# Decoder block on one core: the DMAs of the delta heads' inversion move to GpSimd's queue

## Chip, core and metric

The kernel runs on one core of a Trainium2 chip. The metric is the device time of one execution in microseconds (us), lower is better; a run's number here is a median over runs. TensorE (PE) multiplies, VectorE (DVE), ScalarE (ACT) and GpSimd (POOL) work elementwise, and SyncE (SP) only issues DMAs. Each engine, and each engine's DMA queue, takes its instructions in order.

## What is computed

A decoder block on x of 1024 tokens and 1024 channels in float32: a half step of a gated feed-forward network, a mixer, a second such half step, a final norm. The mixer adds two kinds of attention. The change touches one, the gated delta rule with 8 heads of 128 channels:

```
G = jnp.cumsum(scalar_chunks(g.astype(f32)), axis=-1)
decay = jnp.exp(jnp.where(causal, G[..., :, None] - G[..., None, :], -jnp.inf))
kk = jnp.einsum("bhnid,bhnjd->bhnij", k_beta, k) * decay
M = jnp.eye(CHUNK, dtype=f32) + jnp.where(strict, kk, 0.0)
sol = lax.linalg.triangular_solve(M, rhs, left_side=True, lower=True, unit_diagonal=True)
qk = jnp.einsum("bhnid,bhnjd->bhnij", q, k) * decay
def step(S, xs):
    qdc, qkc, uc, wc, kc, gc = xs
    v_new = uc - jnp.einsum("bhcd,bhdv->bhcv", wc, S)
    o = jnp.einsum("bhcd,bhdv->bhcv", qdc, S) + jnp.einsum("bhij,bhjv->bhiv", qkc, v_new)
    S = S * gc[..., None, None] + jnp.einsum("bhcd,bhcv->bhdv", kc, v_new)
    return S, o
```

The triangular solve is done by inverting M.

## The kernel before

Feed-forward products and projections are three matmuls each of float32 split in a high and a low part (L138, L367). After the first feed-forward step comes the mixer, with the eight delta heads in a loop over i (ORDER gives the head), then the other attention, whose gates also use the delta heads' results (y_d), then the second feed-forward step.

A delta head treats its 1024 tokens as 8 blocks of 128 on the partitions. Its steps, by the names in the code:

- `delta_kq`, `delta_v`: projections of k, q and v with a short convolution. Their matmuls (L138) are the bulk of TensorE's work in a head, and other steps are woven between them.
- `delta_decay`: loads the head's row of cumulated decay from g_d to all partitions (gb, 512 KB, two buffers, by SyncE) and makes from it em, the decay matrix (one buffer). L845 is VectorE's first step that reads gb.
- `delta_prep`: products of k with k and q (L902). VectorE multiplies them with em (L904 gives qk, L908 the triangle, written over em). SyncE stores the 32 x 32 diagonal blocks in l_d (4 DMAs, L914), loads them with one block row per partition as lt (4 DMAs, L917) and loads the identity xp (L919). GpSimd inverts all 32 blocks in 31 steps of two operations (L924, L927), copies the result transposed (xt, L929), and stores xp and xt in x_d (4 DMAs each, L932 and L933).
- `delta_blocks`: SyncE loads the inverses back in place as xb and yb (8 DMAs, L944 and L945).
- `delta_levels`: TensorE joins the 32 x 32 inverses to those of the whole block (L981, L994); it needs xb and yb.
- `delta_rec`: the recurrence over the 8 blocks, with the output norm (`out_rms`, L800 to L806) and the output oT (L1040). L1040 reads a PSUM bank that a later product needs. qsq of L967 belongs to this norm.

The loop works ahead: in turn i it makes em and starts the inversion of head i + 1, and projects k and q of head i + 2. Each engine's order is settled when the program is built, by a scheduler with priorities (the tile framework); around the steps named it follows the order of the code. SyncE's queue holds the loads of projection weights (raw, two buffers, L112), the inversion's loads and stores, gb and the stores of finished heads (y_d) in one line.

Of the kernel before, what the change touches and what calls it, by code (L numbers as in the profile page):

```python
# [15 lines left out]
P = 128  # L16
T = 1024
# [719 lines left out]
def mixer(st, sto, tc, pool, start, xs, load_unit, dense, ptile, bank, rsqrt_newton, split, new_x, accumulate,  # L737
          ounits, dram, pr, ident, ones, cst, eye, wlr, win, wout, y_d, h_d, sqrt_table, strassen_products, wp, psum, divide, recent, pinned, run):
    nc = tc.nc
# [9 lines left out]
    def big(tag, bufs=None, shape=None):  # L749
        p = cur[0] if cur else me if tag in early else mb  # L750
        return p.tile(shape or [P, T], F32, name=tag, tag=tag, bufs=bufs)
# [69 lines left out]
    def delta_kq(i, a, kq=None, steps=None):  # L821
# [12 lines left out]
            conv_silu(U_DK + h, (8 + h) * 4, put(0), (6,), steps)  # L834
        return kq

    def delta_decay(i):
        h = ORDER[i]
        gb = big("gb", 2)
        nc.sync.dma_start(out=gb, in_=g_d[h:h + 1, :].broadcast_to([P, T]))  # L840
        gb4 = gb.rearrange("p (n a i) -> p n a i", n=NCH, a=2)
        gla, glb = gb4[:, :, 0, 63], gb4[:, :, 1, 63]
        db = sp.tile([P, NCH, 2], F32, name="db", tag="db", bufs=2)
        nc.vector.tensor_copy(out=db, in_=ngt[:, h, :].unsqueeze(2).broadcast_to([P, NCH, 2]))
        nc.vector.tensor_add(out=db[0:64, :, 1], in0=db[0:64, :, 1], in1=gla[0:64])  # L845
        kdec = sp.tile([P, NCH], F32, name="kdec", tag="kdec", bufs=2)
        nc.vector.tensor_add(out=kdec, in0=db[:, :, 1], in1=glb)
        nc.scalar.activation(out=kdec, in_=kdec, func=AF.Exp)
        gl = sp.tile([P, NCH], F32, name="glast", tag="glast", bufs=2)
        nc.vector.tensor_add(out=gl, in0=gla, in1=glb)  # L850
        nc.scalar.activation(out=gl, in_=gl, func=AF.Exp)
        em = big("em", 1)
        nc.vector.tensor_tensor(out=em.rearrange("p (m i) -> p m i", i=64),
                                in0=gb.rearrange("p (m i) -> p m i", i=64),
                                in1=db.rearrange("p n a -> p (n a)").unsqueeze(2).broadcast_to([P, 16, 64]),
                                op=ALU.add)
        nc.vector.tensor_tensor(out=v3(em), in0=v3(em), in1=minmask.unsqueeze(1).broadcast_to([P, NCH, P]),
                                op=ALU.min)
        nc.scalar.activation(out=em, in_=em, func=AF.Exp)
        gla_c = sp.tile([P, NCH], F32, name="glac", tag="glac", bufs=2)  # L860
        nc.vector.tensor_copy(out=gla_c, in_=gla)
        nc.vector.tensor_tensor(out=gb4[:, :, 1, :], in0=gb4[:, :, 1, :],
                                in1=gla_c.unsqueeze(2).broadcast_to([P, NCH, 64]), op=ALU.add)
        nc.scalar.activation(out=gb, in_=gb, func=AF.Exp)

        return gb, gl, kdec, em

    def delta_prep(i, kq, kdec, em, res):
        h = ORDER[i]
        kT = kq[:, :, 0, :]  # L870
        kst = big(f"kst{i % 2}", 1)
        ssk = sp.tile([P, NCH], F32, name="ssk", tag="ssk", bufs=2)
        for b in range(2):
            q = bank()
            for n in range(4):
                nc.tensor.transpose(out=q[:, n * P:(n + 1) * P], in_=kT[:, b * 4 + n, :], identity=ident)
            for n in range(4):
                c = b * 4 + n
                jk = sp.tile([P, P], F32, name="jk", tag="jk", bufs=1)
                nc.scalar.activation(out=jk, in_=q[:, n * P:(n + 1) * P], func=AF.Square,  # L880
                                     accum_out=ssk[:, c:c + 1])
            nc.vector.tensor_tensor(out=v3(kst)[:, b * 4:b * 4 + 4, :], in0=q4(q),
                                    in1=kdec[:, b * 4:b * 4 + 4].unsqueeze(2).broadcast_to([P, 4, P]), op=ALU.mult)
        nc.vector.tensor_scalar(out=ssk, in0=ssk, scalar1=EPS, scalar2=None, op0=ALU.add)
        rs = rsqrt_newton(sp, ssk, NCH, "rs", 2)
        cj = sp.tile([P, NCH], F32, name="cj", tag="cj", bufs=2)
        nc.vector.tensor_mul(out=cj, in0=rs, in1=rs)
        nc.vector.tensor_mul(out=cj, in0=cj, in1=beta[:, h, :])
        nc.vector.tensor_mul(out=rs, in0=rs, in1=ssk)

        lt3 = v3(em)
        qk = big(f"qk{i % 2}", 1)
        em3 = v3(em)
        for b in range(4):
            if b % 2 == 0:
                pin = yield
            q = bank()
            q3 = q.rearrange("p (n a i) -> p n a i", n=2, a=2)
            with pinned(pin):
                for n in range(2):  # L900
                    c = b * 2 + n
                    nc.tensor.matmul(out=q[:, n * 256:n * 256 + 256], lhsT=kT[:, c, :],  # L902
                                     rhs=kq[:, c, :, :], start=True, stop=True)
            nc.vector.tensor_tensor(out=v3(qk)[:, b * 2:b * 2 + 2, :], in0=q3[:, :, 1, :],  # L904
                                    in1=em3[:, b * 2:b * 2 + 2, :], op=ALU.mult)
            for n in range(2):
                c = b * 2 + n
                nc.vector.scalar_tensor_tensor(out=lt3[:, c, :], in0=q3[:, n, 0, :], scalar=cj[:, c:c + 1],  # L908
                                               in1=em3[:, c, :], op0=ALU.mult, op1=ALU.mult)
        l_d = dram.tile([32, 32, 32], F32, name=f"l_d{h}")  # L910
        x_d = dram.tile([2, 32, 32, 32], F32, name=f"x_d{h}")
        for b in range(4):
            r = slice(32 * b, 32 * b + 32)
            nc.sync.dma_start(out=l_d[8 * b:8 * b + 8].rearrange("n j i -> j n i"), in_=lt3[r, :, r])  # L914
        lp = big("lt", 1, [P, 32, 32])
        for a in range(4):
            nc.sync.dma_start(out=lp[32 * a:32 * a + 32], in_=l_d)  # L917
        xp = big("xp", 1, [P, 32, 8])
        nc.sync.dma_start(out=xp, in_=eye)  # L919
        for j in range(31):  # L920
            r, m = 31 - j, min(j + 1, 8)
            tmp = mp.tile([P, 256], F32, name="itmp", tag="itmp", bufs=1)
            tv = tmp[:, :r * m].rearrange("p (r c) -> p r c", r=r)
            inv_eng.tensor_tensor(out=tv, in0=lp[:, j, j + 1:].unsqueeze(2).broadcast_to([P, r, m]),  # L924
                                  in1=xp[:, j, :m].unsqueeze(1).broadcast_to([P, r, m]), op=ALU.mult)
            xv = xp[:, j + 1:, :m]
            inv_eng.tensor_tensor(out=xv, in0=xv, in1=tv, op=ALU.subtract)  # L927
        xt = big("xt", 1, [P, 256]).rearrange("p (c i) -> p c i", c=8)
        inv_eng.tensor_copy(out=xt.rearrange("p c i -> p i c"), in_=xp)  # L929
        for a in range(4):  # L930
            r, c = slice(32 * a, 32 * a + 32), slice(8 * a, 8 * a + 8)
            nc.gpsimd.dma_start(out=x_d[0, :, :, c], in_=xp[r])  # L932
            nc.gpsimd.dma_start(out=x_d[1, :, c, :], in_=xt[r])  # L933
        res[i] = (x_d, kst, qk, cj, rs)

    def delta_blocks(em, x_d):
        lt3, n13 = v3(em), v3(n1)
        nc.vector.tensor_copy(out=n13[0:32, :, 32:64], in_=lt3[0:32, :, 32:64])
        nc.vector.tensor_copy(out=n13[64:96, :, 96:128], in_=lt3[64:96, :, 96:128])
        nc.vector.tensor_copy(out=n2, in_=lt3[0:64, :, 64:128])  # L940
        xb3, yb3 = v3(xb), v3(yb)
        for b in range(4):
            r = slice(32 * b, 32 * b + 32)
            nc.sync.dma_start(out=xb3[r, :, r], in_=x_d[0, 8 * b:8 * b + 8].rearrange("n i c -> i n c"))  # L944
            nc.sync.dma_start(out=yb3[r, :, r], in_=x_d[1, 8 * b:8 * b + 8].rearrange("n i c -> i n c"))  # L945

    def delta_v(i, kq, gb, rs, res, steps):
        h = ORDER[i]
# [276 lines left out]
    for b in range(2):  # L1225
        q = bank()
        for n in range(4):
# [5 lines left out]
        nc.vector.tensor_scalar(out=ngt[:, :, b * 4:b * 4 + 4], in0=qv[:, 64:72, :], scalar1=-1.0,  # L1233
                                scalar2=None, op0=ALU.mult)

    gb, gl, kdec, em = delta_decay(0)
    kqs = [kq0]
    preps, vs = {}, {}
# [5 lines left out]
    outs = []  # L1244
    for i in range(8):
        kq, (x_d, kst, qk, cj, rs), gl0 = kqs[i], preps[i], gl
        gb0 = gb
        prep = None
        if i < 7:
            gb, gl, kdec, em = nd  # L1250
            prep = delta_prep(i + 1, kqs[i + 1], kdec, em, preps)
            next(prep)
# [5 lines left out]
            run(v)  # L1258
        qsq, vt3 = vs[i]
        yi = delta_levels()  # L1260
        if i < 7:
            delta_blocks(em, preps[i + 1][0])
        else:
            stl.close()
            stl = ExitStack()
            mx = pool(stl, "mx")
# [4 lines left out]
        for j in GATES[i]:  # L1271
            gate(U_DG + ORDER[j], U_MB + ORDER[j], outs[j])
            nc.sync.dma_start(out=y_d[ORDER[j]], in_=outs[j])
        if i < 4:
            nc.sync.dma_start(out=y_d[ORDER[i]], in_=outs[i])
    sums_own, sums_inplace, strassen = strassen_products(
        mx, xs, lambda: wp.tile([P, 512], F32, name="raw", tag="raw", bufs=2),
        lambda: wp.tile([P, 512], F32, name="raw", tag="raw", bufs=2),
# [167 lines left out]
```

## Time and profile before

| | |
|---|---|
| median of 3 runs | 2672.56 us (2671.76 to 2674.8) |
| the profiled execution | 2674.82 us, of which span 2672.4 |
| TensorE busy | 2503.4 us, 94% |
| VectorE busy | 1869.0 us, 70% |
| GpSimd busy | 1113.9 us, 42% |
| ScalarE busy | 1066.5 us, 40% |
| mean granted clock of TensorE | 0.983 |
| delta heads | from about 750 to 1340 us |

Starts and idle times below are in microseconds from the span's start. "Idle before" names what ended the wait of that engine; a chain of waits is followed back from its end. A DMA's row is its issue, and its landing comes later.

### The profile page before, as it was taken

The numbers are of one execution on the slowest core, as the hardware profiler recorded it, in microseconds if no ns is written. First come the engines' busy times: TensorE is split into PE (matmuls) and PEld (weight loads), VectorE is DVE, ScalarE is ACT, GpSimd is POOL, SyncE is SP. The second block draws the span as 40 slices with busy tenths as digits, with TensorE's granted clock in tenths as the row PEclk, the third lists the DMA queues.
The fourth block names the chain that finished last, engine by engine and source line by source line (L and its number), as shares of the span: only waits on it lengthen the run. The fifth ranks groups of instructions, "written<-read, shape, count | busy, mean of one in ns | idle before, by whom it ended". The sixth has DMA issues, their size and how long they took to land.

```text
span 2672.4 us, 32776 instructions
## 1 busy us (share of the span) xinstructions
PE 2503.4 (94%) x11656; PEld 2019.5 (76%) x11656; DVE 1869.0 (70%) x2907; ACT 1066.5 (40%) x1845; POOL 1113.9 (42%) x1200
## 2 busy tenths in 40 slices
PE   7899999899997988889989999999989999998998
PEld 6788888667776767667767787877768888886677
DVE  8755556999686767667586757766586555558996
ACT  5333334333352434344345544545233333343331
POOL 4544444653327444445452212221154444446541
PEclk9999999999998999999999999999999999999999
DMA  3222221322222222212211212122312222213222
GB/s 114 79 73 82 83 91 60 112 79 91 98 81 52 60 56 59 60 48 56 63 50 37 80 43 84 40 84 87 122 32 76 68 87 87 87 60 115 79 87 80
DMA packets 118051, 199.04 MB, mean 74 GB/s; under 512 B 37208, under 2 KB 43096, under 8 KB 117888
## 3 DMA queue, kind: packets, MB, share of 16 engines
q1 hardware_dynamic: 111376, 184.04, 21.5%
q0 software_dynamic: 4352, 10.49, 1.5%
q10 hardware_dynamic: 2160, 2.43, 0.3%
q8 instruction: 91, 1.49, 0.2%
q14 instruction: 72, 0.59, 0.1%
HBM read 158.73 MB, written 38.17 MB: 74 GB/s over the span
## 4 chain that ended last, share of the span: by engine, by line
PE 60%; DVE 16%; POOL 9%; issue 5%; DMA 4%; ACT 4%; SPq 2%; POOLq 0%; DVEq 0%; ACTq 0%
PE q L367 28%; PE m L367 10%; PE ps L138 10%; PE q L573 6%; POOL xp L927 4%; POOL itmp L924 3%; DVE wl L126 3%; DVE xl L126 1%; DVE ha L578 1%; DVE h L578 1%; PE q L902 1%; PE q L981 1%; DMA s<-a_d 1%; DVE xl L238 1%; DMA gb<-g_d 1%
## 5 line engine op out<-in xcount | busy, mean ns | idle before, releaser
L126 DVE TENSOR_TENSOR wl<-raw,wh 128x512 fp32r<-128x512 f32 x244 | 200.2, 821 | 172.0 <-ACT wh L125 170.5
L138 PE MATMUL ps<-xl,wh 128*128 128x512 f32 (+2 forms) x736 | 254.8, 405 | 20.2 <-ACT wh L119 8.3
L126 DVE TENSOR_TENSOR wl<-sr,wh 128x512 fp32r<-128x512 f32 x232 | 204.7, 882 | 76.2 <-ACT wh L125 75.9
L138 PE MATMUL ps<-xh,wh 128*128 128x512 f32 (+2 forms) x736 | 254.4, 405 | 0.0
L138 PE MATMUL ps<-xh,wl 128*128 128x512 f32 (+2 forms) x736 | 254.2, 403 | 0.1
L367 PE MATMUL q<-xh,wl 128*128 128x512 f32 x640 | 249.4, 390 | 0.0
L367 PE MATMUL q<-xh,wh 128*128 128x512 f32 x640 | 249.3, 390 | 0.0
L367 PE MATMUL q<-xl,wh 128*128 128x512 f32 x640 | 249.2, 389 | 0.0
L125 ACT CAST wh<-sr 128x512 fp32r<-128x512 f32 x232 | 143.7, 619 | 244.7 <-PE q L573 61.9
L924 POOL TENSOR_TENSOR itmp<-lt,xp 128x112 f32<-128x112 f32 (+29 forms) x248 | 114.9, 463 | 255.1 <-DMA lt<-l_d 226.1
L472 POOL TENSOR_TENSOR s<-s,ysc 128x512 f32<-128x512 f32 x80 | 112.6, 1418 | 247.8 <-ACT s L471 247.8
L125 ACT CAST wh<-raw 128x512 fp32r<-128x512 f32 x244 | 144.9, 594 | 176.2 <-PE q L367 100.5
L138 PEld LDWEIGHTS ps<-xl,wh 128*128 128x128 f32 (+1 forms) x736 | 137.8, 191 | 51.7 <-DVE xl L238 9.1
L355 POOL TENSOR_TENSOR raw<-sr 128x512 f32<-128x512 f32 x20 | 27.5, 1375 | 328.6 <-DMA sr<-in_win 235.8
L138 PEld LDWEIGHTS ps<-xh,wh 128*128 128x128 f32 (+1 forms) x736 | 138.8, 192 | 24.6 <-issue 0.8
L138 PEld LDWEIGHTS ps<-xh,wl 128*128 128x128 f32 (+1 forms) x736 | 137.4, 191 | 23.7 <-issue 1.0
L378 DVE TENSOR_TENSOR c<-c,q 128x512 f32<-128x512 f32 x120 | 82.4, 686 | 84.8 <-PE q L367 84.6
L367 PEld LDWEIGHTS q<-xl,wh 128*128 128x128 f32 x640 | 120.2, 188 | 26.2
L367 PEld LDWEIGHTS q<-xh,wl 128*128 128x128 f32 x640 | 120.1, 188 | 25.5
L367 PEld LDWEIGHTS q<-xh,wh 128*128 128x128 f32 x640 | 120.1, 188 | 25.3
L373 ACT COPY c<-q 128x512 f32<-128x512 f32 x120 | 70.5, 588 | 162.2 <-PE q L367 161.7
L927 POOL TENSOR_TENSOR xp<-xp,itmp 128x112 f32<-128x112 f32 (+29 forms) x248 | 120.9, 488 | 19.4
(483 smaller groups left out, 6780.8 us busy)
## 6 DMA issues: line engine op xcount, KB each, us to landing
sr<-in_win SPq DMA_DIRECT2D x80, 256.0 KB, 2.6
a_d<-s SPq DMA_DIRECT2D x36, 512.0 KB, 3.7
raw<-in_win SPq DMA_DIRECT2D x66, 256.0 KB, 2.6
raw<-in_d SPq DMA_DIRECT2D x56, 256.0 KB, 2.6
raw<-in_g SPq DMA_DIRECT2D x48, 256.0 KB, 2.6
s<-a_d SPq DMA_DIRECT2D x24, 512.0 KB, 4.2
sr<-in_u SPq DMA_DIRECT2D x44, 256.0 KB, 2.7
raw<-in_u SPq DMA_DIRECT2D x44, 256.0 KB, 2.6
```

The lines of the kernel that those rows point to most:

```text
L125: a = nc.scalar.copy(out=hi, in_=src)
L126: b = (eng or nc.vector).tensor_sub(out=lo, in0=src, in1=hi.bitcast(F32))
L138: mm = nc.tensor.matmul(out=ps[:m, sl], lhsT=w[:, :m], rhs=x[:, sl], start=(i == 0 and a == 0), stop=(i == n - 1 and a == 2))
L355: nc.gpsimd.tensor_tensor(out=o, in0=a, in1=b, op=op)
L367: nc.tensor.matmul(out=ps, lhsT=p[:, c], rhs=q, start=(first and k == 0 and a == 0), stop=(k == 3 and a == 2), skip_group_check=not first)
L373: marks[0] = nc.scalar.copy(out=t, in_=ps).ins
L378: marks[1] = nc.vector.tensor_add(out=t, in0=t, in1=ps).ins
L472: nc.gpsimd.tensor_mul(out=s, in0=s, in1=y)
L573: nc.tensor.matmul(out=ps, lhsT=p[:, c], rhs=q, start=(first and k == 0 and a == 0), stop=(k == 1 and a == 2), skip_group_check=not first)
L578: nc.vector.scalar_tensor_tensor(out=hd[:, sl], in0=ps, scalar=0.5, in1=hd[:, sl], op0=ALU.mult, op1=ALU.add)
L924: inv_eng.tensor_tensor(out=tv, in0=lp[:, j, j + 1:].unsqueeze(2).broadcast_to([P, r, m]), in1=xp[:, j, :m].unsqueeze(1).broadcast_to([P, ...
L927: inv_eng.tensor_tensor(out=xv, in0=xv, in1=tv, op=ALU.subtract)
```

## The change

- All DMAs around the inversion (l_d, lt, xp, xb and yb) are issued by GpSimd instead of SyncE.
- The partitions of lt, xp and xt are numbered block by block (n, a) instead of part by part (a, n), so the transposed result xt is stored by one DMA of 128 x 1 KB instead of four; xp still takes four. The input eye is laid out to match.
- gb has three buffers. Its load is a function of its own, `load_decay`, called for heads 0 and 1 ahead of the loop and for head i + 2 at the start of turn i.
- The stores of heads 0 to 3 to y_d move from the end of a turn to the next turn, behind `delta_levels`.
- The scratch that the program sets aside for GpSimd's DMAs is set to 2048 bytes.

```
+    def load_decay(i):
+        h = ORDER[i]
+        gbs[i] = big("gb", 3)
+        nc.sync.dma_start(out=gbs[i], in_=g_d[h:h + 1, :].broadcast_to([P, T]))
     def delta_decay(i):
-        gb = big("gb", 2)
-        nc.sync.dma_start(out=gb, in_=g_d[h:h + 1, :].broadcast_to([P, T]))
+        gb = gbs.pop(i)
...
-            nc.sync.dma_start(out=l_d[8 * b:8 * b + 8].rearrange("n j i -> j n i"), in_=lt3[r, :, r])
+            nc.gpsimd.dma_start(out=l_d[8 * b:8 * b + 8].rearrange("n j i -> j n i"), in_=lt3[r, :, r])
...
-            nc.sync.dma_start(out=lp[32 * a:32 * a + 32], in_=l_d)
+            nc.gpsimd.dma_start(out=lp[a::4], in_=l_d)
...
-        nc.sync.dma_start(out=xp, in_=eye)
+        nc.gpsimd.dma_start(out=xp, in_=eye)
...
         for a in range(4):
-            r, c = slice(32 * a, 32 * a + 32), slice(8 * a, 8 * a + 8)
-            nc.gpsimd.dma_start(out=x_d[0, :, :, c], in_=xp[r])
-            nc.gpsimd.dma_start(out=x_d[1, :, c, :], in_=xt[r])
+            nc.gpsimd.dma_start(out=x_d[0, :, :, 8 * a:8 * a + 8], in_=xp[a::4])
+        nc.gpsimd.dma_start(out=x_d[1].rearrange("n (a c) i -> (n a) (c i)", a=4), in_=xt.rearrange("p c i -> p (c i)"))
...
-            nc.sync.dma_start(out=xb3[r, :, r], in_=x_d[0, 8 * b:8 * b + 8].rearrange("n i c -> i n c"))
-            nc.sync.dma_start(out=yb3[r, :, r], in_=x_d[1, 8 * b:8 * b + 8].rearrange("n i c -> i n c"))
+            nc.gpsimd.dma_start(out=xb3[r, :, r], in_=x_d[0, 8 * b:8 * b + 8].rearrange("n i c -> i n c"))
+            nc.gpsimd.dma_start(out=yb3[r, :, r], in_=x_d[1, 8 * b:8 * b + 8].rearrange("n c i -> c n i"))
...
+    load_decay(0)
+    load_decay(1)
...
+        if i < 6:
+            load_decay(i + 2)
...
         yi = delta_levels()
+        if 0 < i < 5:
+            nc.sync.dma_start(out=y_d[ORDER[i - 1]], in_=outs[i - 1])
...
-        if i < 4:
-            nc.sync.dma_start(out=y_d[ORDER[i]], in_=outs[i])
...
-    nc = _bacc.Bacc("TRN2", target_bir_lowering=False, num_devices=1)
+    nc = _bacc.Bacc("TRN2", target_bir_lowering=False, num_devices=1, dynamic_dma_scratch_size=2048)
```

SyncE's queue in the middle of the heads, before: the end of one head's loads of the inverse up to the next head's.

```order
L944 DMA xb<-x_d_7093 32x8x32
L945 DMA yb<-x_d_7093 32x8x32
L919 DMA xp<-in_eye 128x256
L112 DMA raw<-in_win 128x512 x2
L840 DMA gb<-g_d 128x1024
L1275 DMA y_d<-oT 128x1024
L112 DMA raw<-in_win 128x512
L914 DMA l_d_7754<-em 32x8x32 x4
L917 DMA lt<-l_d_7754 32x1024 x4
L112 DMA raw<-in_win 128x512 x3
```

The same queue and place after the change.

```order
L842 DMA gb<-g_d 128x1024
L1271 DMA y_d<-oT 128x1024
L112 DMA raw<-in_win 128x512 x6
L842 DMA gb<-g_d 128x1024
L112 DMA raw<-in_win 128x512
L1271 DMA y_d<-oT 128x1024
```

Only weights, decay rows and stores of finished heads are left in it; the first of these decay rows is for a head that is two turns away.

GpSimd between two inversions, before: the last step of one, its stores, the first steps of the next.

```order
L927 TENSOR_TENSOR xp<-xp,itmp 128x8
L929 COPY xt<-xp 128x32x8
L932 DMA x_d_7093<-xp 1024x1x8
L933 DMA x_d_7093<-xt 32x256
...
L924 TENSOR_TENSOR itmp<-lt,xp 128x31
L927 TENSOR_TENSOR xp<-xp,itmp 128x31
```

After the change, the same place.

```order
L933 TENSOR_TENSOR xp<-xp,itmp 128x8
L935 COPY xt<-xp 128x32x8
L937 DMA x_d_7088<-xp 1024x1x8 x4
L938 DMA x_d_7088<-xt 128x256
L949 DMA xb<-x_d_7088 32x8x32
L950 DMA yb<-x_d_7088 32x8x32
...
L925 DMA xp<-in_eye 128x256
L920 DMA l_d_7746<-em 32x8x32 x4
L923 DMA lt<-l_d_7746 32x1024 x4
L930 TENSOR_TENSOR itmp<-lt,xp 128x31
```

Between the stores of one inverse and the next inversion GpSimd's queue now has the loads of xb and yb (four of each, in turn), xp, l_d and lt.

VectorE around the first read of the decay row (L845 before, L851 after), before and then after.

```order
L805 SCALAR_TENSOR_TENSOR h<-q,h 128x512
L882 TENSOR_TENSOR kst_7643<-q,kdec 128x512
L806 SCALAR_TENSOR_TENSOR h<-h 128x512
L845 TENSOR_TENSOR db<-db,gb 64x8
L904 TENSOR_TENSOR qk_7691<-q,em 128x256
L1040 SCALAR_TENSOR_TENSOR oT<-q,ph,h 128x512
```

```order
L806 SCALAR_TENSOR_TENSOR h<-h 128x512
L910 TENSOR_TENSOR qk_7683<-q,em 128x256
L1045 SCALAR_TENSOR_TENSOR oT<-q,ph,h 128x512
L888 TENSOR_TENSOR kst_7635<-q,kdec 128x512
L890 TENSOR_SCALAR ssk<-ssk 128x8
L910 TENSOR_TENSOR qk_7683<-q,em 128x256
L159 TENSOR_SCALAR rsq<-ssk 128x8
L851 TENSOR_TENSOR db<-db,gb 64x8
```

The read of the decay row moved behind the step that writes oT. TensorE's order in the middle heads is the same but for single projection matmuls.

## Rows read from the trace of the kernel before

**Rows 1.** Waits, 880 to 1310: who waited for whom, us, times, longest.

```profile
DVE db L845 <- DMA gb<-g_d: 27.4, 4, 7.9
PE q L902 <- DVE oT L1040: 26.7, 4, 7.7
```

**Rows 2.** Stretches: busy us (x instructions) by engine, clock, DMA share, GB/s.

```profile
955.00:986.00 31.00, 21.39 (x110) 16.89 (x110) 16.64 (x47) 9.07 (x26) 2.00 (x5) 0.89 0.34 94
986.00:1026.00 40.00, 39.97 (x223) 32.48 (x223) 33.80 (x63) 19.11 (x29) 33.84 (x67) 1.00 0.13 27
```

**Rows 3.** Timeline of SyncE's queue: start, us, line, out<-in.

```profile
955.55 0.34 SPq L944 DMA_DIRECT2D xb<-x_d  x1
...
961.10 0.38 SPq L840 DMA_DIRECT2D gb<-g_d  x1
```

**Rows 4.** Timeline of VectorE, same place; in brackets idle before and releaser.

```profile
957.58 0.68 DVE L806 SCALAR_TENSOR_TENSOR h<-h 128x512 f32<-128x512 f32 x1
966.15 0.16 DVE L845 TENSOR_TENSOR db<-db,gb 64x8 f32<-64x8 f32 x1 [7.89 <-DMA gb<-g_d]
966.24 0.41 DVE L904 TENSOR_TENSOR qk<-q,em 128x256 f32<-128x256 f32 x1
966.57 0.73 DVE L1040 SCALAR_TENSOR_TENSOR oT<-q,ph,h 128x512 f32<-128x512 f32 x1
```

**Rows 5.** Timeline of TensorE, that place and three later heads.

```profile
957.06 1.99 PE L902 MATMUL q<-kq 128*128 128x256 f32 x8 [1.18 <-DVE h L805]
...
967.45 3.75 PE L902 MATMUL q<-kq 128*128 128x256 f32 x8 [7.70 <-DVE oT L1040]
970.64 1.38 PE L138 MATMUL ps<-xh,wh 128*128 128x512 f32 x2
...
976.10 1.05 PE L981 MATMUL q<-xb,n 128*128 128x128 f32 x8
...
1036.69 3.65 PE L902 MATMUL q<-kq 128*128 128x256 f32 x8 [4.95 <-DVE oT L1040]
...
1107.48 3.75 PE L902 MATMUL q<-kq 128*128 128x256 f32 x8 [7.03 <-DVE oT L1040]
...
1178.65 3.75 PE L902 MATMUL q<-kq 128*128 128x256 f32 x8 [6.98 <-DVE oT L1040]
```

**Rows 6.** Chain of waits in one head: start, us, what.

```profile
974.17 2.13 DVE em L908 x8
...
983.71 0.22 POOL itmp L924
...
1029.30 0.45 SPq L945
```

**Rows 7.** Instructions of L932 and L933 (ns min/median/max), landings; DMA issues of xb.

```profile
L932 POOL DMA_DIRECT2D x_d<-xp x32: 759/806/871, 823.8 to 1299.6; - x32
...
DMA to landing us min/median/max: 2.6/2.7/4.4
L933 POOL DMA_DIRECT2D x_d<-xt x32: 502/540/615, 824.6 to 1300.3; - x32
...
DMA to landing us min/median/max: 2.0/2.1/3.9
xb<-x_d SPq DMA_DIRECT2D x32, 32.0 KB, 1.9
```

**Rows 8.** Timeline of TensorE in the first and the second head.

```profile
835.73 2.04 PE L981 MATMUL q<-xb,n 128*128 128x128 f32 x8 [14.41 <-DMA xb<-x_d]
...
894.74 1.99 PE L902 MATMUL q<-kq 128*128 128x256 f32 x8 [2.87 <-DVE h L805]
```

**Rows 9.** Chain of waits in the second head.

```profile
884.76 2.66 DMA raw<-in_win
888.12 0.96 ACT qsq L967
```

**Rows 10.** Timeline of GpSimd in an inversion.

```profile
799.47 2.22 POOL L924 TENSOR_TENSOR itmp<-lt,xp 128x176 f32<-128x176 f32 x1
```

More of the change, by code (lines that the diff above doesn't have):

```diff
@@ L835, in delta_kq @@
         return kq
+    gbs = {}
+    def load_decay(i):
+        h = ORDER[i]
+        gbs[i] = big("gb", 3)
+        nc.sync.dma_start(out=gbs[i], in_=g_d[h:h + 1, :].broadcast_to([P, T]))
     def delta_decay(i):
         h = ORDER[i]
-        gb = big("gb", 2)
-        nc.sync.dma_start(out=gb, in_=g_d[h:h + 1, :].broadcast_to([P, T]))
+        gb = gbs.pop(i)
         gb4 = gb.rearrange("p (n a i) -> p n a i", n=NCH, a=2)
@@ L1402 @@
     cst[:, C_MIN:C_MIN + P] = np.where(idx[None, :] >= idx[:, None], f4(0), f4(NEG))
-    eye = np.ascontiguousarray(np.broadcast_to(np.eye(32, dtype=f4).reshape(32, 4, 8).transpose(1, 0, 2)[:, None],
-                                               (4, 32, 32, 8))).reshape(P, 32, 8)
+    eye = np.ascontiguousarray(np.broadcast_to(np.eye(32, dtype=f4).reshape(32, 4, 8).transpose(1, 0, 2)[None],
+                                               (32, 4, 32, 8))).reshape(P, 32, 8)
     par = np.zeros((P, P_N), f4)
```

## The prediction

> **What bounds the kernel now.** I read the waits first, then the stretches, then the queue in which the wait begins. The mixer takes eight delta heads one after the other, and from the third on they follow each other at about 70 us. The PE starts of the second L902 group in four successive heads, 967.45, 1036.69, 1107.48 and 1178.65, are 69.24, 70.79 and 71.17 apart, 70.4 in the mean [rows 5]. In each such head there is a stretch in which TensorE works 40 of 40 us, and one in which it works only 21.4 of 31 at a granted clock of 0.89, partly at 1.2 instead of 2.4 GHz [rows 2]. The waits say why: VectorE waited 27.4 us in 4 heads for the decay row (gb<-g_d), and TensorE 26.7 us in the same 4 heads for oT of L1040 [rows 1].
>
> The place is 955 to 968 us. SyncE's queue is in order. Its loads of xb and yb wait for the head's inverse to land, so the first leaves at 955.55. Only behind these eight, one load of xp and two of raw does the decay row leave, at 961.10 [rows 3]. VectorE, also in order, is free at 958.26 but has L845 next, which reads that row: it idles 7.89 us, until 966.15 [rows 4]. Behind it stands L1040, which frees the PSUM bank for the second group of L902, so TensorE stands 7.70 us. The groups of the four heads waited 7.70, 4.95, 7.03 and 6.98, together 26.7 [rows 5]. L902 feeds the triangular block (em), which goes to GpSimd for the next inversion. One inverse therefore starts the next one, through SyncE's queue.
>
> **The change part by part.** *The decay row* gets a third buffer and a load two heads ahead, and SyncE's queue holds no xb, yb, l_d, lt or xp any more. A row that left 5 us too late now leaves most of a head (some 60 us) early, and 60 us hide its transfer. This takes 26.7 us of waiting away. What is late next at this place: from 958.26 VectorE has L904 and L1040 left ahead of TensorE's second group (its L845 stands behind both in the new order, which takes it off this path too). Before, L904 began at 966.24 and L1040 ended at 967.30 [rows 4], about 1.1 us for the two, so now they would end near 959.4, while TensorE is ready at 967.45 - 7.70 = 959.75. I book 0 to 0.5 us per head as remaining wait and take the upper end, +2 for four heads.
>
> *The clock.* Behind each gap the eight L902 took 3.75, 3.65, 3.75 and 3.75 us; behind a gap of 1.18 they took 1.99. The pair of L138 behind them was slow too, 1.38 us [rows 5]. The excess of the L902 alone is 14.9 - 4 x 1.99 = 6.9 us. Without the gaps the granted clock should stay where it is in the busy stretch, at 1.00, which is 2.4 GHz [rows 2]. I take -7.
>
> *SyncE's raw loads* no longer queue behind xb and yb. In the second head TensorE waited 2.87 us ahead of L902 where the next waits 1.18 [rows 5, 8], and there ScalarE's qsq, ahead of the output norm that TensorE waits for, came right behind such a raw load [rows 9]; -1.7. The stores of y go one head later in a queue that has nothing urgent behind them: 0, hidden by the weight tiles that lie ready (raw has two buffers); uncovered, one would hold a weight load as in the second head, 1.7 us.
>
> *GpSimd's queue.* This is the price. Per head it loses 3 stores (four stores of xt become one) and gains 17 loads and stores: 8 of xb and yb, 4 of l_d, 4 of lt, 1 of xp. Issues that GpSimd already does took 0.81 (x_d<-xp, 1024 pieces) and 0.54 us (x_d<-xt), landing 2.7 and 2.1 us after issue [rows 7]. The moved ones are of 32 x 8 or of 32 pieces, nearer to x_d<-xt; I take 0.60, against some 0.45 on SyncE. The inverse's way in before: em complete at 974.17 + 2.13 = 976.30, inversion begins 983.71, last yb issued 1029.30, landed 1.9 later at 1031.2, 54.9 us in all [rows 6, 7]. Now: 16 issues on the way x 0.15 = +2.4, three landings together +1.0, stores of x_d 4 x 0.81 + 0.54 = 3.8 instead of 5.4, -1.6. That is 56.7 us, +1.8.
>
> How much may it be? The head's levels (L981) need xb. A head without gap and slow clock lasts 70.4 - 26.7/4 - 7/4 = 62.0 us. L981 starts 976.10 - 967.45 = 8.65 after L902, 6.9 without the slow clock, and em is complete 8.85 or 7.1 after it. So L981 comes 62.0 + 6.9 - 7.1 = 61.8 us after em, and the 56.7 fit with 5.1 us to spare. GpSimd's own round fits too: after the last yb it waits for the next em. Work that hides the +1.8 is thus TensorE's projections; if it grew past 5.1 more, every head would pay the rest.
>
> The first head has no such cover: TensorE stood 14.41 us for xb there [rows 8], so that head pays the +1.8 in full. Bounds for the way: -1.6 (issues and landings cost as on SyncE) to +10.8 (below).
>
> Sum: -26.7 - 7 - 1.7 + 2 + 1.8 = **-31.6 us**. Against the profiled execution's 2674.8 that is 2643.2. The median of the runs is 2672.6, 2.2 lower, so I say **2641**.
>
> **The rivals.**
>
> *Stores wait for room.* The diff sets a scratch for GpSimd's DMAs to 2048 bytes, and the four x_d<-xp stores have 1024 pieces of 32 bytes each. No row shows one store waiting for another: before, they were issued back to back. If each waits until the one ahead has landed, three waits of 2.7 - 0.8 = 1.9 add 5.7 us; the spare 5.1 swallows nearly all in heads 3 to 7 (0.6 x 5 = 3), the first head pays 5.7: -31.6 + 8.7 = -22.9, so 2650. With the longest landing seen, 4.4 [rows 7], it is 3 x 3.6 = 10.8: 5 x 5.7 + 10.8 = 39, +7.7, so 2680. Decisive is 9.5 us per head: 5 x (9.5 - 5.1) + 9.5 = 31.6.
> The Trainium skill speaks for this rival. Its page "DMA: Bandwidth & Descriptors" (sections "Terms" and "SWDGE vs HWDGE vs iDMA") has GpSimd's DMAs write 16-byte descriptors to rings in a reserved part of SBUF. An estimate from that page: 2048 bytes hold 128, a store of 1024 pieces over 16 engines puts 64 and one more on each, and two stores do not fit. By the rule the time is that of this rival; no run here shows it yet.
>
> *GpSimd issues slowly beside a busy VectorE* (slower than before). VectorE worked 33.8 of 40 us beside the inversion [rows 2], and one tensor operation of GpSimd stretched to 2.22 us [rows 10]. If the 16 moved issues were stretched by 0.6 us each beyond my 0.60, the 9.5 us are reached and the gain is gone; at 0.9 each, 14.4 us, it is 5 x 9.3 + 14.4 - 31.6 = +29, so 2702. Against it: the 32 issues of x_d<-xp lay between 759 and 871 ns, with VectorE at work [rows 7].
> The Trainium skill has this trap: "SBUF — State Buffer", section "A bandwidth-pool intuition that's wrong (but worth ruling out)", tells of a GpSimd DMA of about 620 ns that took about 3100 beside a VectorE copy. An estimate by that page, 2.5 us more for each of 16, is 40 us per head and far slower than before; the trace's 871 at most speaks against it here.
>
> *The wait only changes its name.* If something else ends where gb ended, such as a late raw load or the output norm's chain on ScalarE (L805, 1.18 us now), TensorE's gaps stay. It would have to be 5 us late or more, which no row there shows. The time is then that of before less at most 5, so 2668 to 2673.
>
> **How the numbers follow.** Forecast 0.60. Stores wait for room, in its mild form, 0.20; the slow issue or the stores at the long landing, slower than before, 0.13; the wait renamed 0.07. Most that can be had is 26.7 + 7 + 1.7 + 1.6 with no new wait, 37 us: 2635; a little more, if the faster queue frees other waits, gives 2632 as the low end. The high end 2662 takes in the mild rival to twice its loss (-11). Of the forecast's chance this range holds 0.58, of the mild rival's 0.20, of the renamed wait's 0.01: 0.79. A measurement of this kernel tells about 0.2%, some 5 us, from no change. Faster by more: 0.60 + 0.20 and 0.01 of the renamed wait, 0.81; within: 0.06; slower: 0.13.
>
> **What would show it.** Right: VectorE's wait for gb and TensorE's for oT gone, L902 at about 2.0 us in all heads, successive L902 some 62 apart, no wait of L981 for xb beyond the first head, there 14 to 17 us. The rival of the full scratch would show as x_d<-xp issues 2 us or more apart, the slow issue as xb and yb issues above 1 us, and both as a wait of L981 for xb in every head. If the head's period is 62 and the total is not near 2641, the loss lies outside the heads: there the order of work is the same but for some 20 matmuls at the program's very start, which I cost at 0 within 2 us.

## The result, and the profile after

The changed kernel takes **2660.0 us** (median; 2655.1 to 2663.7) against 2672.2 of the kernel before, run beside it: a ratio of 0.9946, interval 0.9926 to 0.9965. It is faster by 12 us, where 31.6 were forecast. Its profiled execution took 2661.6, with a span of 2659.8.

The wait that the prediction began with is gone. Waits of the changed kernel, 880 to 1310 us: who waited for whom, us, times, longest.

```profile
POOL x_d L937 <- issue: 53.7, 21, 4.3
...
PE q L908 <- DVE h L805: 6.7, 6, 1.3
...
PE q L986 <- DMA xb<-x_d: 4.7, 3, 2.1
```

Neither VectorE's wait for gb nor TensorE's for oT is among them any more [rows 1]. L908 (the L902 of before) waits only 0.8 to 1.3 us for the output norm, much as before. But GpSimd's x_d<-xp, which had waited once, for 0.31 us, now waits 53.7 us in 7 heads, and L986 (the L981 of before) waits for xb in three. The stretches that answer to [rows 2]: busy us by engine, granted clock, DMA share, GB/s.

```profile
955.00:986.00 31.00, 29.70 (x161) 23.99 (x160) 23.79 (x60) 14.14 (x33) 14.72 (x29) 1.00 0.33 85
986.00:1026.00 40.00, 39.24 (x225) 32.14 (x224) 32.99 (x64) 18.00 (x28) 33.02 (x67) 1.00 0.14 40
```

TensorE works 29.7 of 31 us where it worked 21.4, and the clock is 1.00 instead of 0.89, so wholly at 2.4 GHz. TensorE's timeline, which answers to [rows 5] and [rows 8]: the first L908, the first head's L986, then the second L908 group of four successive heads.

```profile
770.30 1.97 PE L908 MATMUL q<-kq 128*128 128x256 f32 x8
...
848.84 2.04 PE L986 MATMUL q<-xb,n 128*128 128x128 f32 x8 [20.91 <-DMA xb<-x_d]
...
973.68 1.89 PE L908 MATMUL q<-kq 128*128 128x256 f32 x8
...
1036.03 1.89 PE L908 MATMUL q<-kq 128*128 128x256 f32 x8
...
1100.33 1.89 PE L908 MATMUL q<-kq 128*128 128x256 f32 x8
...
1163.54 1.97 PE L908 MATMUL q<-kq 128*128 128x256 f32 x8
```

The groups take 1.89 to 1.97 us and stand 62.4, 64.3 and 63.2 apart, 63.3 in the mean, against 70.4. The first head lost: L908 starts 6 us later than before (764.25), and L986 waits 20.91 us instead of 14.41. So the difference of the two spans, -12.6, has three parts. Up to the first L986 the changed kernel is 848.84 - 835.73 = 13.1 us late. From there to the L986 of the eighth head (1303.68; before 1320.38) it gains 29.8. From there to the end it loses 4.1.

What the stores of x_d do, GpSimd's timeline in a middle head; in brackets the idle time before:

```profile
1025.20 0.84 POOL L937 DMA_DIRECT2D x_d<-xp  x1
1028.27 0.77 POOL L937 DMA_DIRECT2D x_d<-xp  x1 [2.22 <-issue]
1031.34 0.78 POOL L937 DMA_DIRECT2D x_d<-xp  x1 [2.30 <-issue]
1034.81 0.77 POOL L937 DMA_DIRECT2D x_d<-xp  x1 [2.69 <-issue]
1035.57 0.56 POOL L938 DMA_DIRECT2D x_d<-xt  x1
```

Each takes 0.8 us, as before [rows 7], but ahead of the second to the fourth GpSimd stands idle 2.2 to 2.7 us, with no releaser that the profile shows ("issue").

The decay row, counted in order. The fifth of the eight rows, and VectorE's first read of it, in the changed kernel:

```profile
899.89 0.33 SPq L842 DMA_DIRECT2D gb<-g_d  x1
```

```profile
908.22 0.16 DVE L851 TENSOR_TENSOR db<-db,gb 64x8 f32<-64x8 f32 x1
```

Before, the fifth row left at 961.10 and was read at 966.15 [rows 3, 4]. Both have moved a head forward, and the read does not wait. So at the same place of a head VectorE now reads the row of one head later than before. Of the last four reads two stand behind oT's step (L1045) and two ahead of it (1034.63 against 1035.04, and 1098.92 against 1099.34); none waits.

### The profile page after: what moved, and what is told of

Read it like the earlier page. It is cut to its first block, busy times and chain, and to the rows that moved or that the text cites. A ratio compares the mean times of both kernels' runs of the same rounds, so it can differ in the third digit from the quotient of the medians.

```text
span 2659.8 us, 32713 instructions
## 1 busy us (share of the span) xinstructions
PE 2505.2 (94%) x11656; PEld 2020.1 (76%) x11656; DVE 1872.5 (70%) x2907; ACT 1069.3 (40%) x1847; POOL 1177.3 (44%) x1312
## 4 chain that ended last, share of the span: by engine, by line
PE 66%; DVE 15%; POOL 5%; ACT 5%; issue 4%; DMA 2%; DVEq 0%; POOLq 0%; ACTq 0%
PE q L367 28%; PE ps L138 13%; PE m L367 10%; PE q L573 6%; DVE wl L126 2%; PE q L986 2%; DVE xl L126 1%; POOL itmp L930 1%; POOL xp L933 1%; DVE ha L578 1%; DVE h L578 1%; DMA s<-a_d 1%; ACT L803 1%; PE q L908 1%; DVE c L378 1%
## 5 line engine op out<-in xcount | busy, mean ns | idle before, releaser
L373 ACT COPY c<-q 128x512 f32<-128x512 f32 x120 | 70.4, 587 | 162.2 <-PE q L367 161.8
L933 POOL TENSOR_TENSOR xp<-xp,itmp 128x112 f32<-128x112 f32 (+29 forms) x248 | 120.0, 484 | 19.4
```

Of the source, the lines that this page charges most:

```text
L373: marks[0] = nc.scalar.copy(out=t, in_=ps).ins
```

## The experiments

Each ratio is to the kernel before, run beside it; the starts and the period are of the one profiled execution. "First L902" and "first L981" are the starts of TensorE's first product of the first head and of that head's levels, whatever their line in the kernel; the period is the mean distance of the four groups above. The reserve is the scratch that the program sets aside for GpSimd's DMAs. The kernel before sets none and has the default; the Trainium skill gives it as 16 KiB per partition ("SBUF — State Buffer", section "SBUF size: 192, 224, or 256?"). No run here measures that figure, but it fits e5, e6 and e10: there the reserve and an unused tile add up to 16384 bytes, and the order of work is that of the kernel before.

| kernel | reserve | first L902 | first L981 | period | time | ratio and interval |
|---|---|---|---|---|---|---|
| before | default | 764.25 | 835.73 | 70.4 | 2672 to 2675 | 1 |
| changed | 2048 | 770.30 | 848.84 | 63.3 | 2660.0 | 0.9946 (0.9926 to 0.9965) |
| e12 changed, again | 2048 | 772.29 | 850.83 | 63.7 | 2661.3 | 0.9941 (0.9923 to 0.9959) |
| e1 changed, room | 12288 | 774.06 | 846.71 | 62.2 | 2644.9 | 0.9891 (0.9874 to 0.9909) |
| e4 and scans first | 12288 | 769.33 | 846.03 | 65.8 | 2652.8 | 0.9919 (0.9901 to 0.9936) |
| e6 changed, old order | 2048 | 762.39 | 839.40 | 63.7 | 2652.1 | 0.9914 (0.99 to 0.9929) |
| e10 changed, old order | 4096 | 764.16 | 835.56 | 62.1 | 2639.1 | 0.9866 (0.9846 to 0.9885) |
| e5 changed, old order, room | 12288 | 768.21 | 839.23 | 62.2 | 2640.0 | 0.9872 (0.9855 to 0.989) |
| e2 before, small reserve | 12288 | 770.91 | 844.16 | 70.4 | 2686.2 | 1.004 (1.0026 to 1.0055) |
| e3 before, changed reserve | 2048 | 771.47 | 849.75 | 75.7 | 2731.4 | 1.0211 (1.0192 to 1.0231) |
| e7 decay row only | 12288 | 765.94 | 836.93 | 67.9 | 2666.0 | 0.9965 (0.9951 to 0.9978) |
| e8 inversion's DMAs on SyncE | 12288 | 763.68 | 833.43 | 66.8 | 2673.5 | 0.9994 (0.9983 to 1.0005) |
| e9 move only | 12288 | 763.59 | 834.59 | 62.1 | 2636.5 | 0.9856 (0.9838 to 0.9874) |
| e11 decay row on ScalarE | 12288 | 765.00 | 835.80 | 64.8 | 2650.4 | 0.9907 (0.989 to 0.9923) |

### Room for the stores: e1, e3, e10

```
 e1, from the changed kernel
-dynamic_dma_scratch_size=2048
+dynamic_dma_scratch_size=12288
 e3, from the kernel before
-nc = _bacc.Bacc("TRN2", target_bir_lowering=False, num_devices=1)
+nc = _bacc.Bacc("TRN2", target_bir_lowering=False, num_devices=1, dynamic_dma_scratch_size=2048)
```

> The changed kernel with 12288 bytes of reserve for GpSimd's DMAs instead of 2048; no instruction moves against the changed kernel. Theory A (the stores of x_d wait for room): the four x_d<-xp stores leave about 0.8 us apart as before, instead of 3; the first head's wait for xb falls from 20.9 us to about 14.5, the waits of the other heads (1.6, 2.1, 1.1) to near 0; the time falls by 6.4 + up to 5, so to 2649 to 2654. Rival B (the stores are slow for another reason, VectorE's work beside them or the xt store): they stay 2 to 4 us apart and the time stays at 2660. In both cases the first head's preparation stays 6 to 7 us later than in the kernel before.

GpSimd's timeline in a middle head of e1, and its first L986:

```profile
1020.35 3.17 POOL L937 DMA_DIRECT2D x_d<-xp  x4
1023.46 0.60 POOL L938 DMA_DIRECT2D x_d<-xt  x1
```

```profile
846.71 2.04 PE L986 MATMUL q<-xb,n 128*128 128x128 f32 x8 [14.57 <-DMA xb<-x_d]
```

The four stores are back to back again, the first head's wait is 14.57 as it was before [rows 8], no later L986 waits for xb, and the time is 15 us less than the changed kernel's. Theory A holds, at more than its price (6 to 11 us).

> The kernel before with 2048 bytes of reserve; instruction for instruction the order of the kernel with 12288. Theory A (a store of 1024 pieces waits until the one ahead of it has left the ring): its x_d<-xp stores leave 2 to 4 us apart instead of 0.8, some 5 to 7 us more per head, and since the decay row waits behind the inverse in SyncE's queue, each of the heads 3 to 7 and the first pays it in full: six times 6, so 36 us over the kernel with 12288, 2705 to 2725. Rival B (the reserve's size has no effect on the stores): the time of the kernel with 12288. Rival C (the waits are hidden behind GpSimd's own work): under 10 us more.

The kernel before, with no other difference but the reserve, gets the same idle times, in GpSimd's timeline of e3:

```profile
1043.77 0.79 POOL L932 DMA_DIRECT2D x_d<-xp  x1
...
1046.76 0.76 POOL L932 DMA_DIRECT2D x_d<-xp  x1 [1.71 <-issue]
...
1049.72 0.75 POOL L932 DMA_DIRECT2D x_d<-xp  x1 [1.71 <-issue]
...
1052.70 0.76 POOL L932 DMA_DIRECT2D x_d<-xp  x1 [1.73 <-issue]
```

With the x_d<-xt between them the stores again stand 3.0 us apart. There the inverse is on the path of every head, so the period grows by 5.3 us and the time by 45 over e2, which differs from it by the reserve alone. Stalls of the same kind cost the changed kernel 15 us. Theory A holds, at more than its price: 36 us and 2725 at most were expected, 45 and 2731 came.

> The changed kernel in the old order with 4096 bytes of reserve (and an unused tile of 12288). Theory A (a store takes room in the reserve in proportion to its pieces and gives it back when they have left; 2048 bytes hold one store of 1024 pieces and not two): 4096 hold two or three, so one or two of a head's four x_d<-xp stores wait about 2 us instead of three, and the time lies between 2640 and 2652, 2642 to 2648. Rival B (any reserve below the one that holds all four costs the same, since the store waits for an empty ring): three waits as with 2048, 2650 to 2654.

GpSimd's timeline in a middle head of e10:

```profile
1009.02 2.41 POOL L938 DMA_DIRECT2D x_d<-xp  x3
1012.06 0.78 POOL L938 DMA_DIRECT2D x_d<-xp  x1 [0.63 <-issue]
```

With 4096 bytes three stores go at once and only the fourth waits, 0.63 us; the time is that of e5, below the range that theory A gave. So the number of stores that fit grows with the reserve. The fourth's short wait suggests that room comes back while the stores run, which no run tested by itself. The Trainium skill fits this: in "DMA: Bandwidth & Descriptors", sections "Terms" and "SWDGE vs HWDGE vs iDMA", GpSimd's DMAs write descriptors of 16 bytes to rings in SBUF. By an estimate from that page a store of 1024 pieces over 16 engines needs 65 places in each, so 128 places (2048 bytes) hold one store, 256 hold three and 768 all four. The traces agree: one store, three stores and four stores went without a wait (but for one of 0.2 us in e1).

### The order of work in the first head: e2, e4, e5, e6, e12

> The kernel before with 12288 bytes of reserve instead of the 16384 it has; nothing else. The reserve lies in SBUF, and with less of it the order of the instructions comes out another way: VectorE's scans of the decay (L773) stand interleaved with the convolution of the next unit, as in the changed kernel. Theory A (this order, not GpSimd's new work, makes the first head's preparation late): the first L902 starts 5 to 7 us later than 764 us, the heads' period stays 70 us, and the time is 2676 to 2679. Rival B (the lateness comes of the moved DMAs or of the decay's early loads): the first L902 stays at 764 and the time at 2672.

e2 is the kernel before with 12288 bytes of reserve. TensorE's first L902, and the second group that waited in [rows 5]:

```profile
770.91 1.97 PE L902 MATMUL q<-kq 128*128 128x256 f32 x8
...
974.09 3.75 PE L902 MATMUL q<-kq 128*128 128x256 f32 x8 [6.35 <-DVE oT L1040]
```

L902 is 6.7 us late, as in the changed kernel, though no DMA moved and VectorE waits for gb in every such head as before. Theory A holds, and the price is higher than its 4 to 7: 11 us by the medians. The profiled execution shows 4.7 of them; where the rest lies was not seen. What differs with the reserve is seen early at ScalarE. Its timeline near the start of the program in the changed kernel, and the same steps in the kernel before:

```profile
4.56 0.28 ACT L764 ACTIVATE ph<-pr 128x96 f32<-128x96 f32 x1 [2.54 <-DMA pr<-in_par]
...
4.94 1.28 ACT L1214 ACT_TABLE_LOAD   x1
```

```profile
738.48 0.28 ACT L764 ACTIVATE ph<-pr 128x96 f32<-128x96 f32 x1
...
738.86 1.28 ACT L1209 ACT_TABLE_LOAD   x1
```

Our reading is that the size of the reserve, which is taken from SBUF, moves the tiles there. The mixer's constants (ph, nea, masks) would then have shared their place with a tile of the first feed-forward step before, and could only be made at 738 us; with a smaller reserve they lie in free space, are made at once, and everything that the scheduler orders behind them comes out a little differently. That the size alone brings the new order is shown by e2. That it does so through the place of tiles is argued: an unused tile undoes it in e5 below, but no trace shows where a tile lies. VectorE's last scan of the decay (L773), before and after:

```profile
762.31 0.47 DVE L773 TENSOR_TENSOR_SCAN yi<-cs,oT 8x64 f32<-8x64 f32 x2
```

```profile
769.55 0.28 DVE L773 TENSOR_TENSOR_SCAN yi<-cs,oT 8x64 f32<-8x64 f32 x1
```

Before, twelve of the sixteen scans ran in one piece; now at most six do, and the others stand singly or in twos between steps of the convolution (L791) of the next unit. The first head waits for the last of them: TensorE turns the scans' result just ahead of the first L908, and g_d is stored behind them (at 769.86 against 762.80 before) and gb loaded from there. TensorE in the changed kernel:

```profile
769.89 0.33 PE L1234 MATMUL q<-cs,yi 128*128 128x128 f32 x1 [0.18 <-DVE yi L773]
...
770.30 1.97 PE L908 MATMUL q<-kq 128*128 128x256 f32 x8
```

In thirteen of the fourteen kernels the first inversion begins 24.4 to 25.4 us after the last scan has ended, whichever order they have. The exception is e4.

> The kernel with 12288 bytes of reserve and, in it, the decay of the heads (its scans, L773, and what leads to them) ahead of the convolution in VectorE's and ScalarE's order; nothing is left out. Theory A (the first head is late because the scans wait behind the convolution): the first L908 starts at 764 us or earlier instead of 770, and with the stores back to back the first head's wait for xb is near the 14.4 us of before; the time is 5 to 8 us below that of the kernel with 12288 alone, 2642 to 2648. Rival B (TensorE or the loads of the weights set the first head's start): L908 starts at 770 as before and the time does not move by more than 2 us.

```
 e4, from e1
+    with tc.high_priority(offset=400):
         nc.scalar.activation(out=sm[32:40], in_=sm[32:40], func=AF.Tanh, scale=0.5)
...
         seg_scan(sm[64:72], gtm, ones[64:72, :64])
```

This brought the first L908 forward by 4.7 us, but the first L986 by 0.7 only, the period rose to 65.8, and the kernel is 8 us slower than e1. Neither theory forecast that. The scans do end at 764.1 instead of 773.6, but VectorE puts other steps ahead of the triangle of the first head, L914, which begins at 784.45 against 786.0 in e1. A priority given to one chain moved others too; why the later heads got longer was not followed up.

> The changed kernel with 12288 bytes of reserve and an unused tile of 4096 bytes per partition beside ha, so that the mixer's constants lie again where they wait for a tile of the stage before; the scans L773 and all of the first head's preparation stand in the order of the kernel before. Theory A (the reserve's size costs the changed kernel twice, by stores that wait and by an order that starts the first head late): the first L908 is back near 764 us (774.06 in the kernel with 12288 alone), the heads' period stays 62, and the time is 6 to 11 us below that kernel's 2645: 2634 to 2639, which is the 2641 of the prediction or a little less. Rival B (the late first head is taken up later by work that hides it): 2643 to 2647.

> The changed kernel with its 2048 bytes of reserve and an unused tile of 14336 bytes beside ha; instruction for instruction the order of the kernel with 12288 bytes and the old order. Theory A: the stores of x_d wait again (2 to 4 us apart), the first L908 is near 764; the time is 9 to 16 us above the kernel with 12288 and the old order, 2646 to 2652, and 6 to 11 below the changed kernel. Rival B (order and stores are not separate: an early first head only waits longer): 2656 to 2662.

```
 e5 and e6, from the changed kernel (e6: 3584 columns, and the reserve stays 2048; e10: 3072 and 4096)
         ha = hp.tile([P, KT, T], F32, name="ha")
+        spare = hp.tile([P, 1024], F32, name="spare")
...
-dynamic_dma_scratch_size=2048
+dynamic_dma_scratch_size=12288
```

In our reading the unused tile pushes the first step's tiles up, so that the constants share a place again. What the trace shows is that ph is made late again and the first head's scans stand as before. e5, ScalarE's and TensorE's timeline:

```profile
742.45 0.28 ACT L765 ACTIVATE ph<-pr 128x96 f32<-128x96 f32 x1
```

```profile
839.23 2.05 PE L987 MATMUL q<-xb,n 128*128 128x128 f32 x8 [15.29 <-DMA xb<-x_d]
...
962.40 1.89 PE L909 MATMUL q<-kq 128*128 128x256 f32 x8
...
1148.92 1.97 PE L909 MATMUL q<-kq 128*128 128x256 f32 x8
```

Its time is 2640.0, just above theory A's range and below B's, and its first L902 came at 768.21, not at 764; e6 is at 2652.1, at the edge of A's. The four kernels make a square. Room is worth 0.0055 in the new order (changed to e1) and 0.0042 in the old (e6 to e5), 15 and 11 us. The old order is worth 0.0032 without room (changed to e6) and 0.0019 with it (e1 to e5), 9 and 5 us. The 5 us alone lie within the two intervals; the order's price is clearest in e2 against the kernel before. The changed kernel ran again beside others:

> The changed kernel itself beside the others. If the two prices (stores that wait, late first head) add up, it is the time with room and old order, 2640, plus 12 for the stores plus 5 to 8 for the order: 2657 to 2661, as measured first.

It came out at 2661.3, 0.3 us above that range; the square's own prices, 11 to 15 and 5 to 9, give 2656 to 2664. One execution says less than the medians: with the old order the first L902 started between 762.4 and 768.2 in eight kernels, with the new between 770.3 and 774.1 in five.

### Which part of the change frees the heads: e7, e8, e9, e11

All four have 12288 bytes and the unused tile, and their first heads scan in the old order.

> The kernel before with the decay row alone changed: three buffers, loaded two heads ahead; the inversion's loads stay on SyncE, the eight stores of x_d and the eye as before; 12288 bytes of reserve and the unused tile, which leave the order of before. Theory A (the decay row's lateness is all that the heads lose, as the terms -26.7, -7 and +2 of the sum have it): VectorE's wait for gb is gone, the heads' period falls from 70 to about 62, the time is 30 to 35 us below before, 2638 to 2644 where before takes 2672 to 2675. Rival B (behind SyncE's long queue the weight tiles of raw come late instead, so the wait is renamed and the moved DMAs are needed): period 65 to 70, 2655 to 2672.

> The changed kernel without its new decay row: two buffers and the load where it stood before, at its use; the inversion's DMAs stay on GpSimd; 12288 bytes of reserve and the unused tile, so the old order. Theory A (what made the decay row late is SyncE's queue alone: with the inversion's DMAs off it the row leaves in time even from two buffers): the heads' period is 62 and the time within 4 us of the kernel that has both, 2637 to 2644. Rival B (the row then waits for its buffer instead, so the third buffer is needed too): VectorE still waits 3 us or more per head for gb, period 65 or more, 2652 to 2665.

```
 e7, from the kernel before
+        gbs[i] = big("gb", 3)
+        nc.sync.dma_start(out=gbs[i], in_=g_d[h:h + 1, :].broadcast_to([P, T]))
...
+        if i < 6:
+            load_decay(i + 2)
 e9, from the changed kernel
-        gb = gbs.pop(i)
+        gb = big("gb", 2)
+        nc.sync.dma_start(out=gb, in_=g_d[h:h + 1, :].broadcast_to([P, T]))
```

e7, SyncE's queue, then VectorE and TensorE at the same place:

```profile
956.95 0.34 SPq L951 DMA_DIRECT2D xb<-x_d  x1
...
962.64 0.38 SPq L843 DMA_DIRECT2D gb<-g_d  x1
```

```profile
967.09 0.17 DVE L852 TENSOR_TENSOR db<-db,gb 64x8 f32<-64x8 f32 x1 [7.57 <-DMA gb<-g_d]
```

```profile
968.39 3.75 PE L909 MATMUL q<-kq 128*128 128x256 f32 x8 [7.38 <-DVE oT L1047]
```

This is [rows 3] to [rows 5] over again, with three buffers. The load stands earlier in the program, but in SyncE's queue it is still behind xb, yb and raw, and it is read 4.5 us after it leaves. e7 gains 9 us, so rival B's range, though the wait kept its name (3 heads instead of 4).

There is a second cause in it. The row shown is the sixth; the kernel before reads the fifth at this place. In e7 the fifth had left and been read a head earlier. The sixth is read here in a small first step, for which VectorE waits; em, the decay matrix, is made from it only at 1061.64, 95 us later. The fifth row's load, its first read, and em's step on the sixth:

```profile
892.45 0.33 SPq L843 DMA_DIRECT2D gb<-g_d  x1
```

```profile
899.27 0.16 DVE L852 TENSOR_TENSOR db<-db,gb 64x8 f32<-64x8 f32 x1
...
1061.64 1.21 DVE L860 TENSOR_TENSOR em<-gb,db 128x1024 f32<-128x1024 f32 x1
```

So the rows did leave a head earlier, but VectorE's small first read of each moved forward with them. Whether three buffers alone would do with that read left in its place, no run shows. e9 has two buffers and the load where it was, and only the inversion's DMAs are off the queue:

```profile
950.95 0.33 SPq L841 DMA_DIRECT2D gb<-g_d  x1
```

```profile
958.27 0.15 DVE L846 TENSOR_TENSOR db<-db,gb 64x8 f32<-64x8 f32 x1
```

The row leaves as soon as L968, the last reader of its buffer, has ended (948.89 + 2.02 = 950.91), 7.3 us before it is read, and nobody waits. In the kernel before the buffer of this row, the fifth there too, was free at 953.45, but the row left at 961.10, behind the inverse's loads:

```profile
951.43 2.02 DVE L968 TENSOR_TENSOR kq<-kq,gb 128x1792 f32<-128x1792 f32 x1 [0.27 <-ACT qsq L967]
```

At this place L846 stands behind L1040, which could by itself keep TensorE from waiting. A head later it stands ahead of L1040, as L845 did before, and still does not wait, so the row's time is enough:

```profile
1018.67 0.16 DVE L846 TENSOR_TENSOR db<-db,gb 64x8 f32<-64x8 f32 x1
...
1019.08 0.73 DVE L1040 SCALAR_TENSOR_TENSOR oT<-q,ph,h 128x512 f32<-128x512 f32 x1
```

The period is 62.1 and the time **2636.5**, so theory A holds, half a us below its range. It is the lowest of all, though its interval overlaps those of e5 and e10. With the queue emptied the third buffer shows no gain.

> The changed kernel with the inversion's l_d, lt, xp, xb and yb back on SyncE, all else as changed (one store of xt, the eye's new rows, the decay row), with 12288 bytes and the unused tile. It differs from the kernel with the decay row alone in the single store of xt. Theory A (the move to GpSimd brings nothing of its own once the decay row is early): within 3 us of the kernel with the moved DMAs, room and the old order, 2636 to 2642. Rival B (the move is worth something by SyncE's raw loads): that kernel is 4 us or more faster than this one.

Rival B holds: e8 is 33 us slower than e5. ScalarE's wait for weight tiles in it, 880 to 1310:

```profile
ACT wh L119 <- DMA raw<-in_win: 16.4, 3, 8.5
```

Behind the inversion's DMAs the weight tiles come late as well as the row (VectorE still waits for gb, 15.2 us in 3 heads). That is the rival "the wait only changes its name", for a kernel that leaves the DMAs on SyncE. Why e8 is slower than e7 was not settled; besides the stores of xt they differ in the numbering of lt, xp and xt and in where y_d is stored.

> The kernel before with the decay row in three buffers, loaded from ScalarE's queue instead of SyncE's; every DMA of the inversion stays where it was before; 12288 bytes and the unused tile. Theory A (the kernel with the decay row alone gained little because in SyncE's queue, which is in order, the row still stood behind xb and yb): from another queue it leaves early, VectorE's wait for gb is gone, the period is about 62, and the time 2640 to 2648. Rival B (the weight tiles behind xb and yb are the next to be late, or ScalarE's queue holds the row as long): period 66 or more, 2655 to 2672.

```
 from e7
-        nc.sync.dma_start(out=gbs[i], in_=g_d[h:h + 1, :].broadcast_to([P, T]))
+        nc.scalar.dma_start(out=gbs[i], in_=g_d[h:h + 1, :].broadcast_to([P, T]))
```

Between the theories: 2650.4, period 64.8. VectorE's wait for gb falls from 19.9 us in e7 to 4.4. ScalarE's queue and VectorE:

```profile
962.91 0.33 ACTq L843 DMA_DIRECT2D gb<-g_d  x1
```

```profile
962.22 0.75 DVE L1047 SCALAR_TENSOR_TENSOR oT<-q,ph,h 128x512 f32<-128x512 f32 x1
...
968.19 0.17 DVE L852 TENSOR_TENSOR db<-db,gb 64x8 f32<-64x8 f32 x1 [1.74 <-DMA gb<-g_d]
```

The row is little earlier: it leaves 0.7 us after VectorE has ended the output norm (3.1 in e7) and is read 5.3 us later. But here its read stands behind L1047, so oT, and TensorE with it, no longer wait for it. e11 changed the queue and VectorE's order at once and doesn't separate them; that the emptied queue is enough is shown by e9. And raw still waits behind xb and yb (ACT for raw 13.5 us in 6 times). The kernel with the row's load on ScalarE is 25 us faster than before (0.0093), the one with all the others moved 38 (0.0144).

## Why the prediction was right or wrong

The step that failed is the first head's term, +1.8, which measured +13.1. About 6.3 us of that are stores that wait for room, where the sum took them as back to back; 6.0 are a late start, from an order of work that the text put at 0 within 2 us. Both come of the 2048 bytes, and the stores lengthen the later heads by 1.1 us each as well. The 2660.0 lies inside the stated range, 2632 to 2662, only because its high end was widened for the rival of the full scratch; the sum did not foresee it.

*The gap, the clock, the raw loads* (-26.7, -7, -1.7, +2; together -33.4): right. Between the first and the eighth head's L981 the changed kernel gains 29.8 us, and 36.0 once the stores don't wait (e5: 1287.89 - 839.23 against 1320.38 - 835.73). The period was forecast at 62.0; it is 62.2 in e1 and e5.

*What makes the row early*: half right. The text put it on the third buffer and the load two heads ahead, together with the emptied queue. By e9 the emptied queue is enough. And the row is not "some 60 us" early: in the changed kernel the fifth row leaves 61 us earlier than before, but its first read moved forward by 58, and the last four rows are read 4.7 to 8.3 us after they leave.

*The price of an issue on GpSimd* (0.60 us): right. xb and yb took 0.58, l_d 0.58, lt 0.53. The inverse's way in e1, from em complete at 974.29 + 2.16 to the last yb's landing (issued 1030.37, landing 2.1 later), is 56.0 us, forecast 56.7. "GpSimd issues slowly" is out: in the changed kernel no moved issue took over 0.62 us, in e1 none over 0.71. The 3100 ns that the Trainium skill's "SBUF — State Buffer", section "A bandwidth-pool intuition that's wrong (but worth ruling out)", tells of for a GpSimd DMA beside a VectorE copy were not met here.

*The first head* (+1.8): wrong, as said. The 6.3 are its wait for xb of 20.91 against 14.57 in e1, the 6.0 the first L908 at 770.30 against 764.25, each by one execution.

*"Stores wait for room" at 0.20*: the wrong choice. It was named with its place, its size of 1.9 us per wait (measured 2.2 to 2.7 in the shown head, up to 4.3) and its time, 2650; e6, which has this fault alone, took 2652. What spoke against it, that the stores were back to back before, was no evidence, because the kernel before ran without the 2048 bytes; with them (e3) it has the idle times too. The slack of 5.1 us per head was about right and a little small: 53.7 us of waiting in 7 heads, 7.7 each, lengthen the period by 1.1 us, where 5.1 of slack would leave 2.6.

*Order "the same but for some 20 matmuls at the program's start", 0 within 2 us*: wrong. It cost 5 to 9 us by the ratios. The text looked at the orders around the middle heads; on VectorE the scans of the decay had moved in the first head, which has no cover. And the mover is a line that the prediction read only as a limit on DMAs; e2 shows that its size alone changes the order.

*After the heads*: 4.1 us more than before. No cause was found: from the eighth head's L981 to the end the kernels took 1349 to 1358 us, e1 with the changed kernel's very order 1350.1 against 1356.1.

So the sum -31.6 was near for the edits that it priced: without the two costs of the 2048 bytes (e5) the kernel is 2640.0, a ratio of 0.9872, some 34 us below before. The changed kernel gives back 11 to 15 us to the stores and 5 to 9 to the order.

## What to carry to other kernels

For a load that comes late, look at what is ahead of it in its queue before adding buffers or asking for it earlier, and look where its first reader stands: a scheduler may move the read forward with the load. A reserve or a limit in the diff is to be held against the largest burst of the kernel, and a trace taken with a larger one says nothing against it. A change of SBUF sizes can reorder work far from the edit: compare the order on every engine in the stretch that has no cover, not where the edit is.

## What was not expected of the hardware

- A store of 1024 pieces by GpSimd needs room in the reserve: with 2048 bytes each further one waits 1.7 to 2.8 us as a rule (up to 4.3), with 4096 three go at once and the fourth waits 0.6 to 0.7, with 12288 they go back to back, with one idle time of 0.2 us. The profile calls that wait "issue".
- Stalls of this kind cost 15 us where the inverse had slack in most heads (changed kernel against e1) and 45 where it had none (e3 against e2).
